# An early jump in VectorE's program and another order of GpSimd's last waits, in a layer norm that is bound by its transfers

## Chip, cores, metric

One core of one Trainium2 chip. The metric is the device time of one execution in microseconds (us), lower is better. All executions named here were fast, with a granted clock of 1.0.

## The reference

```python
def setup_inputs():
    batch, seq, dim = 32, 512, 1024
    return {"x": np.random.randn(batch, seq, dim).astype(np.float32), "eps": 1e-5}

def reference(x, eps):
    mean = np.mean(x, axis=-1, keepdims=True)
    var = np.var(x, axis=-1, keepdims=True)
    return ((x - mean) / np.sqrt(var + eps)).astype(np.float32)
```

16,384 rows of 1,024 floats: 67 MB are read and 67 MB are written.

## The kernel before

The rows go through a ring of 48 row slots in each partition, in 17 tiles (15 of 8 rows, then 6 and 2). SyncE issues the loads (ScalarE that of half the first tile), VectorE takes each row's statistics, GpSimd combines them, ScalarE takes the root, normalizes in place and issues the store. A load into a ring place waits for the store of the tile that was there. VectorE's program is three tiles, a loop of six tiles that runs twice, and the rest:

```python
    nc.vector.memset(eps_t[:], eps_val)
    nc.vector.memset(power[:], -1.0)
    for t in range(FIRST):                      # FIRST = 3
        vector(t, 16, 1)                        # 16 bn_stats and a reciprocal
    turn = nc.vector.alloc_register("turn")
    nc.vector.reg_mov(turn, 1)
    nc.vector.addr_align(128, max_nops=0)
    with nc.vector.Fori(16, 16 * TURNS + 1, 16) as arrived:
        for t in range(FIRST, FIRST + SLOTS):   # 6 tiles, TURNS = 2
            vector(t, nc.vector.lower_val(arrived), turn)
        nc.vector.reg_add(turn, turn, 1)
    for t in range(FIRST + TURNS * SLOTS, len(plan)):
        vector(t, 16, 1)
    ...
    for t in range(len(plan)):
        if t in owner.values():
            nc.gpsimd.wait_ge(stored[t], sixteens(stored, t))
```

`addr_align(n, max_nops=0)` asks that the next instruction be loaded at a multiple of n instruction slots. The gap is not filled with no-ops; a branch leads over it (in the trace of before, one COMPARE_BRANCH of VectorE's sequencer at 52.46 us, 41 ns long). The last lines are the end of the kernel: GpSimd waits for the stores that nobody else has waited for.

## Time and profile before

| | before |
|---|---|
| time, median of the first 3 runs | 318.04 us (317.63 to 318.19) |
| span of the profiled run | 316.04 us |
| time less span | 1.84 us |
| moved by DMA | 134.2 MB, 425 GB/s |
| 8 KB instruction packets in the span | 3 |
| last store: first and last of its 16 parts land | 313.67, 314.96 us |

The page counts 16 DMA engines, and the trace has 16 landing records for each transfer; I read them as one part on each engine. A wait is over with the last of the 16: of the load that the first statistics wait for, the first part landed at 12.85 us, the fifteenth at 13.36 and the last at 13.72, and the statistics start at 13.75. So one late part is enough to delay a tile.

### The profile page before, as it was taken

Reading aid. Unit: us, or ns where it says so; the run is one execution under the profiler, and the core shown is the slowest. Engines: PE = TensorE matmul, PEld = TensorE weight load, DVE = VectorE, ACT = ScalarE, POOL = GpSimd, SP = SyncE. Lnnn points to the kernel's source line nnn. Section 1 sums busy time; section 2 is a strip of 40 time slices with the busy share of each in tenths; the row PEclk is TensorE's granted clock in tenths of the full one; section 3 lists DMA queues with packets and bytes.
Section 4 is the critical chain, followed back from the end, with each engine's and each line's share of the span. In section 5 each row is a group of like instructions: output and inputs, shape, how many; then the busy total and the mean of one; then the engine's idle time right before and its main releaser. Section 6 shows DMA issues by size and latency. Waiting matters only on the chain.

```text
span 316.0 us, 713 instructions
## 1 busy us (share of the span) xinstructions
DVE 156.4 (49%) x273; ACT 153.0 (48%) x146; POOL 41.7 (13%) x176
## 2 busy tenths in 40 slices
DVE  0296595956191651907529084380934709283000
ACT  1006695865834709256091651907429083383800
POOL 0002202022002020020200202011020110204300
DMA  7999999999999999999999999999999999999996
GB/s 294 435 460 402 452 406 402 461 398 465 399 466 402 460 415 448 431 431 452 411 456 406 456 406 456 406 460 402 464 402 460 406 441 452 429 434 425 448 399 285
DMA packets 5043, 134.24 MB, mean 425 GB/s; under 512 B 560, under 2 KB 560, under 8 KB 560
## 3 DMA queue, kind: packets, MB, share of 16 engines
q10 hardware_dynamic: 2592, 69.21, 50.9%
q1 hardware_dynamic: 2448, 65.01, 47.9%
q14 instruction: 3, 0.02, 0.0%
HBM read 67.11 MB, written 67.11 MB: 425 GB/s over the span
## 4 chain that ended last, share of the span: by engine, by line
DMA 61%; DVE 18%; ACT 9%; POOL 5%; issue 2%; ACTq 0%; DVEq 0%; POOLq 0%; SPq 0%
DMA ring<-in_x_dram 32%; DMA out_dram<-ring 29%; DVE stats L119 17%; ACT ring L215 9%; POOL rstd L187 1%; POOL dev L177 1%; POOL dev L181 1%; ACT std L205 0%; POOL dev L173 0%; POOL nmean L170 0%; POOL dev L174 0%; POOL half L166 0%; POOL half L182 0%; POOL nmean L167 0%; POOL ss L183 0%
## 5 line engine op out<-in xcount | busy, mean ns | idle before, releaser
L119 DVE BATCH_NORM_STATS2 stats<-ring 128x6 f32<-128x512 f32 x256 | 153.5, 677 | 86.1 <-DMA ring<-in_x_dram 85.5
L215 ACT ACTIVATE ring<-ring,nmr,rstd 128x1024 f32<-128x1024 f32 x128 | 146.6, 1226 | 11.2 <-POOL nmr L190 11.2
L205 ACT ACTIVATE std<-ss,eps_t 128x8 f32<-128x8 f32 (+2 forms) x17 | 5.1, 300 | 135.1 <-POOL ss L183 134.7
L166 POOL TENSOR_TENSOR half<-stats 128x16 f32<-128x16 f32 (+2 forms) x17 | 4.0, 233 | 232.3 <-DVE stats L119 232.3
L130 DVE RECIPROCAL rstd<-std 128x8 f32<-128x8 f32 x15 | 3.0, 203 | 48.5 <-ACT std L205 48.5
L177 POOL TENSOR_SCALAR dev<-dev 128x32 f32<-128x32 f32 (+2 forms) x17 | 5.0, 295 | 1.5
L190 POOL TENSOR_TENSOR nmr<-nmean,rstd 128x8 f32<-128x8 f32 (+2 forms) x17 | 3.5, 205 | 9.9 <-DVE rstd L130 9.7
L181 POOL TENSOR_TENSOR dev<-dev,stats 128x32 f32<-128x32 f32 (+2 forms) x17 | 4.3, 255 | 1.4
L173 POOL TENSOR_TENSOR dev<-stats,nmean 128x32 f32<-128x32 f32 (+2 forms) x17 | 4.1, 241 | 1.4
L174 POOL TENSOR_TENSOR dev<-dev 128x32 f32<-128x32 f32 (+2 forms) x17 | 4.0, 237 | 1.3
L170 POOL TENSOR_SCALAR nmean<-nmean 128x8 f32<-128x8 f32 (+2 forms) x17 | 4.0, 235 | 1.5
L182 POOL TENSOR_TENSOR half<-dev 128x16 f32<-128x16 f32 (+2 forms) x17 | 3.7, 215 | 1.3
L167 POOL TENSOR_TENSOR nmean<-half 128x8 f32<-128x8 f32 (+2 forms) x17 | 3.4, 202 | 1.3
L183 POOL TENSOR_TENSOR ss<-half 128x8 f32<-128x8 f32 (+2 forms) x17 | 3.4, 202 | 1.3
L187 POOL TENSOR_TENSOR rstd<-std,power 128x6 f32<-128x6 f32 (+1 forms) x2 | 2.1, 1042 | 3.0 <-ACT std L205 3.0
L205 ACT ACT_TABLE_LOAD x1 | 1.3, 1283 | 1.3 <-SPq L55 1.3
L134 DVE MEMSET eps_t<- 128x1 f32 x1 | 0.1, 59 | 1.0 <-SPq L55 1.0
L251 POOL MEMSET const-float32-0.0<- 128x1 f32 x1 | 0.1, 99 | 0.2 <-issue 0.2
L251 POOL MEMSET const-bfloat16-1.0<- 128x1 bf16 x1 | 0.1, 102 | 0.0
L251 POOL MEMSET const-uint8-127<- 128x1 uint8 x1 | 0.1, 102 | 0.0
L251 POOL MEMSET const-float32-1.0<- 128x1 f32 x1 | 0.1, 99 | 0.0
L135 DVE MEMSET power<- 128x8 f32 x1 | 0.1, 65 | 0.0
## 6 DMA issues: line engine op xcount, KB each, us to landing
out_dram<-ring ACTq DMA_DIRECT2D x15, 4096.0 KB, 46.4
ring<-in_x_dram SPq DMA_DIRECT2D x14, 4096.0 KB, 45.5
ring<-in_x_dram SPq DMA_DIRECT2D x1, 3072.0 KB, 43.1
out_dram<-ring ACTq DMA_DIRECT2D x1, 3072.0 KB, 16.0
ring<-in_x_dram ACTq DMA_DIRECT2D x1, 2048.0 KB, 12.6
ring<-in_x_dram SPq DMA_DIRECT2D x1, 2048.0 KB, 12.8
ring<-in_x_dram SPq DMA_DIRECT2D x1, 1024.0 KB, 54.8
out_dram<-ring ACTq DMA_DIRECT2D x1, 1024.0 KB, 14.3
```

The costliest lines, as they stand in the source:

```text
L119: i = nc.vector.bn_stats(out=stats[:, at + k, s, :], in_=ring[:, at + k, s * BN_MAX : (s + 1) * BN_MAX],)
L166: then(0, g.tensor_tensor(out=h, in0=mean4[:, :, 0:2], in1=mean4[:, :, 2:4], op=ALU.add))
L170: g.tensor_scalar(out=nm, in0=nm, scalar1=-1.0 / H, scalar2=None, op0=ALU.mult),
L173: then(3, g.tensor_tensor(out=d, in0=mean4, in1=spread, op=ALU.add))
L174: then(4, g.tensor_mul(out=d, in0=d, in1=d))
L177: g.tensor_scalar(out=d, in0=d, scalar1=float(D // H), scalar2=None, op0=ALU.mult),
L181: then(6, g.tensor_tensor(out=d, in0=d, in1=m2, op=ALU.add))
L182: then(7, g.tensor_tensor(out=h, in0=d[:, :, 0:2], in1=d[:, :, 2:4], op=ALU.add))
L187: i = g.tensor_tensor(out=r, in0=std_t, in1=power[:, :K], op=ALU.pow)
L190: then(10, g.tensor_mul(out=nmr[:, at : at + K], in0=nm, in1=r), own)
L205: nc.scalar.activation(out=std[:, at : at + K], in_=ss[:, at : at + K], func=AF.Sqrt, bias=eps_t[:], scale=1.0 / D,)._wait_ge(*summed[t]). ...
L215: i = nc.scalar.activation(out=ring[:, k, :], in_=ring[:, k, :], func=AF.Identity, bias=nmr[:, k : k + 1], scale=rstd[:, k : k + 1],).then ...
```

## The change

The intent: VectorE's code is moved to a multiple of 64 slots at the very start, while VectorE has no data (in before it is idle there for 12.64 us). And the wait for the last store is put on GpSimd's last branch, so that no further instruction follows that landing.

```diff
     nc.vector.memset(eps_t[:], eps_val)
     nc.vector.memset(power[:], -1.0)
+
+
+    nc.vector.addr_align(64, max_nops=0)
     for t in range(FIRST):
         vector(t, 16, 1)
...
-    for t in range(len(plan)):
+    for t in reversed(range(len(plan))):
         if t in owner.values():
             nc.gpsimd.wait_ge(stored[t], sixteens(stored, t))
```

## The prediction

> **What bounds the kernel now.** I read the profile's page first, to see which resource is full. Its busy shares, its DMA row, its queues and its groups of instructions give this:
>
> ```profile
> DVE 156.4 (49%) x273; ACT 153.0 (48%) x146; POOL 41.7 (13%) x176
> ...
> DMA  7999999999999999999999999999999999999996
> ...
> q14 instruction: 3, 0.02, 0.0%
> HBM read 67.11 MB, written 67.11 MB: 425 GB/s over the span
> ...
> L119 DVE BATCH_NORM_STATS2 stats<-ring 128x6 f32<-128x512 f32 x256 | 153.5, 677 | 86.1 <-DMA ring<-in_x_dram 85.5
> ```
>
> No engine is busy for half of the span. The 16 DMA engines are at nine tenths or more in 38 of 40 slices, and 134.2 MB at 425 GB/s are 315.8 us, the whole span of 316.0. VectorE's statistics wait 85.5 us for loads. So the transfers bound the kernel. A change of the program text that moves no byte can gain only before the queues are full, after the last byte, or where it lets the queues run dry. The diff touches VectorE's code position and GpSimd's last waits, so I looked at three places: VectorE's start, its way into its loop, and the end.
>
> The timeline of the first 16 us:
>
> ```profile
> 0.93 0.37 SPq L96 DMA_DIRECT2D ring<-in_x_dram  x1
> 1.01 0.06 DVE L134 MEMSET eps_t<- 128x1 f32 x1 [1.01 <-SPq L55]
> 1.04 0.07 DVE L135 MEMSET power<- 128x8 f32 x1
> ...
> 13.75 2.47 DVE L119 BATCH_NORM_STATS2 stats<-ring 128x6 f32<-128x512 f32 x4 [12.64 <-DMA ring<-in_x_dram]
> ```
>
> The new jump will stand between the second and third of these VectorE rows: 12.64 us of idle time that a load ends.
>
> The chain of waits around the way into the loop, from the third reciprocal to the statistics of tile 3 (L140 is the alignment that the kernel already has, seen as a branch of the sequencer DVEq):
>
> ```profile
> 52.36 0.06 DVE rstd L130
> 52.42 0.03 issue
> 52.46 0.04 DVEq L140
> 52.50 0.49 issue
> 52.99 0.04 DVEq L141
> ...
> 53.15 9.60 DVE stats L119 x16
> ```
>
> The branch is recorded for 0.04 us, and nothing follows it for another 0.49. That is the one visible cost of code position. What it costs the kernel is told by the timeline after it, at the next tile:
>
> ```profile
> 65.98 0.20 DVE L130 RECIPROCAL rstd<-std 128x8 f32<-128x8 f32 x1 [3.24 <-ACT std L205]
> ...
> 66.95 1.29 DVE L119 BATCH_NORM_STATS2 stats<-ring 128x6 f32<-128x512 f32 x2 [0.76 <-DMA ring<-in_x_dram]
> ```
>
> VectorE waits again, 0.76 us, for the load of tile 4, whose last part landed at 66.92.
>
> The end, from the queries by source line (columns: shortest/median/longest ns, first and last start). L234 holds GpSimd's waits for the stores, L55 the branch out of the kernel's block and the signal after it:
>
> ```profile
> L234 POOLq EVENT_SEMAPHORE  x3: 42/43/43, 305.3 to 315.0; - x3
> ...
> L55 POOLq COMPARE_BRANCH  x1: 38/38/38, 315.1 to 315.1; - x1
> L55 POOLq NOP  x1: 17/17/17, 315.2 to 315.2; - x1
> ```
>
> In the records with three decimals: the last store's last part lands at 314.957, the third wait is recorded at 314.980, the branch at 315.067, the signal at 315.238, and the closing barriers end at 316.04.
>
> [...]ScalarE's stores land in the order of issue, each about 19.3 us after the one before in the steady part (98.89, 118.23, 137.57 us). [...] The trace shows three instruction packets inside the span, of 8,192 bytes each in the packet records, at 57.1, 84.5 and 94.3 us. It shows none at the branch of 52.46, so it does not show that this branch waited for such a fetch. [...]from a branch's start to the next recorded instruction it is 206 ns at VectorE's back edge (157.285 to 157.491) and 536 ns at L140 (52.456 to 52.992). The measured ones are used. [...]
>
> **The change part by part.** The built programs differ in just two places, line numbers aside.
>
> *VectorE.* One alignment to 64 slots is added after the two memsets; by the title it becomes one taken branch. No work moves between engines. Added cost: one branch, 0.2 to 0.54 us by the two measured ones, say 0.54, at about 1.1 us. It ends near 1.7 us, and the data comes at 13.72. Even if the target must be fetched, and if that took 5 us on full queues (a guess well beyond the 0.3 us that a packet takes), 7 us would remain. On the path: 0. Possible gain: code ahead of the loop now begins on a multiple of 64, and it is 51 instructions of tiles 0 to 2 and one register move. It ends about 12 slots short of the next multiple of 64, so the second branch skips a dozen slots[...]. If it falls from 536 ns to the back edge's 206, tile 3 starts 0.33 us earlier; if nothing changes, 0. Where does 0.33 us go? Tile 3's reciprocal moves from 65.98 to 65.65, then tile 4 still waits for its load until 66.92: VectorE's own gain ends there, and 0.76 us idle become 1.09. ScalarE's tile 3 ends 0.33 us earlier, so its store is issued at 75.36 and not 75.69. But the store of tile 2 was issued at 62.07 and lands at 98.89[...]: 23 us of slack against 0.33. The store's landing (118.23), which releases the load of tile 9, does not move. On the path: 0.
>
> *GpSimd.* The same seven waits, in the other order. They are packed two to a semaphore instruction, the seventh on the branch. Before, in pairs: tiles 14 and 13; 15 and 12; 16 and 11; on the branch tile 10. After: 12 and 13; 11 and 14; 10 and 15; on the branch tile 16. Before, the last landing releases the third semaphore instruction at 314.980 and the branch starts 87 ns later. After, the three semaphore instructions are through once tile 15's store has landed (312.53), 2.4 us ahead of the end, and the landing releases the branch itself. Removed from the path: 315.067 - 314.980 = 0.087 us, with nothing beside it, for all engines wait there. Nothing is added unless a waiting branch leaves later than one that finds its semaphore set. GpSimd's first branch, which waited too, took 153 ns to the next record (0.744 to 0.897); the last one, which did not, 171. So no penalty shows.
>
> Sum: 0 - 0.087 = -0.09 us. From 318.04 that is 317.95 us, 0.03% less.
>
> **The rivals.** (a) *The branch's stall does reach the end.* Then up to 0.33 us come on top, or 0.67 if tile 3 followed as closely as tile 1 did (119 ns from its reciprocal's start to its first statistics, against 789 at tile 3): 317.3 to 317.6. For it: the chain of waits runs through these rows. Against it: the chain follows releasers backwards and does not show slack, and the two slacks above (0.76 us on VectorE, 23 us in the store queue) are both larger than the gain. (b) *The new position costs something.* A fetch might now fall where VectorE is needed, for instance at the second branch or at the loop's exit. If it added one more 0.54 us at 52 us, the 0.76 us before tile 4 would still swallow it. At the loop's exit the wait for the next load is 3.94 us. Time unchanged, 317.95; only several us at once could show, up to 319. (c) *Code position outside the span.* The time is 317.88 where the span is 316.04; 1.8 us are not seen, and code at the end of VectorE's program lies elsewhere after the change. A few tenths either way: 317.6 to 318.4. (d) *Transfers fall differently.* [...] That would be a few tenths, of either sign.
>
> **Range and chances.** The three runs before lie between 317.63 and 318.19, a spread of 0.56 us that is six times my effect. The median of the runs after may be off by 0.3 us from this alone[...]; rival (a) widens the low side and (b), (c) the high side. I take 317.4 to 318.5. Two per cent are 6.4 us, more than all the terms together, so faster or slower by that much is 1% each.
>
> **What would show it.** Right: an early branch of VectorE near 1.1 us with the first statistics still at 13.7 and released by the load; tile 4's statistics still started by its load near 66.9 whatever the way into the loop costs; the store of tile 3 landing near 118.2; the last wait record some 2.4 us before the last landing and the branch within 30 ns after it; from landing to span's end 1.00 us in place of 1.09. Wrong: tile 9's load landing earlier by as much as the branch got shorter (then rival a); the first statistics later than 13.8 (then the fetch did not hide); a DMA row with slices below nine in the middle; or a time below 317.4 in repeated pairs of runs.

## The result, and the profile after

| | before | after |
|---|---|---|
| time, median of 6 runs | 317.78 us | 318.48 us |
| range | 317.63 to 318.19 | 317.94 to 319.39 |
| ratio of the fast runs | | 1.0021, 95% interval 1.0004 to 1.0039 |
| span of the profiled run (its time) | 316.04 (317.88) | 317.57 (319.39) |
| 8 KB instruction packets in the span | 3 | 4 |
| last store: first and last part land | 313.67, 314.96 | 313.65, 316.56 |

A ratio is the mean time of one kernel's fast runs over that of the other's in the same rounds, so it is not quite the ratio of the medians. The change is slower by 0.2%, and its runs spread 1.45 us where those of before spread 0.56. The profiled execution of after is its slowest, so the 1.5 us between the two spans is the largest case and not the mean; the mean is 0.0021 x 317.8 = 0.7 us.

The page of after, the rows of the DMA engines, of the instruction queue and of the statistics:

```profile
DMA  7999999999999999999999999999999999999995
...
q14 instruction: 4, 0.03, 0.0%
HBM read 67.11 MB, written 67.11 MB: 423 GB/s over the span
...
L119 DVE BATCH_NORM_STATS2 stats<-ring 128x6 f32<-128x512 f32 x256 | 153.5, 677 | 87.6 <-DMA ring<-in_x_dram 87.1
```

No work on an engine grew. VectorE waits 87.1 us for loads where it waited 85.5. There is one more instruction packet. Where it is, the DMA view of after, restricted to the first 14 us, says (the same view of before has no q14 row):

```profile
## 3 DMA queue, kind: packets, MB, share of 16 engines
q1 hardware_dynamic: 175, 3.11, 52.3%
q10 hardware_dynamic: 144, 2.10, 39.9%
q14 instruction: 1, 0.01, 0.1%
```

The timeline of after at the start, then the query of L138, the new alignment (shortest/median/longest ns, first and last start):

```profile
1.04 0.07 DVE L135 MEMSET power<- 128x8 f32 x1
...
14.30 1.88 DVE L119 BATCH_NORM_STATS2 stats<-ring 128x6 f32<-128x512 f32 x3 [13.19 <-DMA ring<-in_x_dram]
```

```profile
L138 DVEq COMPARE_BRANCH  x1: 47/47/47, 1.0 to 1.0; - x1
```

The jump is at 1.03 us as intended, and the first statistics are still started by the load. But that load is late: its last part lands at 14.28 us where it landed at 13.72, while the first part lands at 12.95 against 12.85. One part of the 16 is late: behind the first there are 0.36 us to the fifteenth and 1.32 to the sixteenth (before: 0.51 and 0.88).

The way into the loop, in the chain of after, and tile 4's start in its timeline:

```profile
52.92 0.06 DVE rstd L130
52.98 0.04 issue
53.01 0.04 DVEq L143
53.05 0.46 issue
53.52 0.04 DVEq L144
...
53.68 9.60 DVE stats L119 x16
```

```profile
67.73 1.88 DVE L119 BATCH_NORM_STATS2 stats<-ring 128x6 f32<-128x512 f32 x3 [1.02 <-DMA ring<-in_x_dram]
```

The second branch costs what it cost (0.50 us from its start to the next record, 0.54 before), and tile 4 is still started by its load.

The last 18 us in the DMA view, before and then after (40 slices of 0.45 us from 300 us on; the second row is GB/s):

```profile
DMA  9599195193939393939393926999962000000000
GB/s 874 218 510 583 73 874 218 73 728 164 710 164 710 164 710 164 710 164 710 164 710 164 710 109 291 455 401 401 473 291 91 36 0 0 0 0 0 0 18 0
```

```profile
DMA  9899899779969595959595959699973200000000
GB/s 437 364 510 510 364 510 437 328 328 401 492 291 601 218 655 218 655 218 655 218 655 218 655 218 401 273 473 382 492 310 146 91 18 18 36 18 0 0 0 0
```

The full rates end near the same place. After the change four slices follow with 18, 18, 36 and 18 GB/s: single packets of 8 KB, one after the other. I read this as one DMA engine that still has its part of the last store to write while fifteen are done: 15 of the 16 parts have landed by 314.85 us (before 314.66), the last lands at 316.56. (The lone 18 near the end of the row of before is an instruction packet at 317.2 us, after the span.)

GpSimd's end, from the queries by line:

```profile
L237 POOLq EVENT_SEMAPHORE  x3: 43/7212/7218, 299.6 to 306.9; - x3
...
L55 POOLq COMPARE_BRANCH  x1: 38/38/38, 316.6 to 316.6; - x1
```

Each of these instructions waits for two stores (two semaphores in its record). The last of the three now starts at 306.9 and ends with its second store's landing at 314.11, and the last landing at 316.564 releases the branch itself at 316.588. From landing to the span's end it takes 1.001 us, before 1.087. This part works, and is worth 0.086 us.

**Following one DMA engine.** The records give each packet's start, duration, size and queue, but not its DMA engine. I sorted the packets into 16 sequences, with two demands: the next packet of a sequence starts about 3 ns before the end of the last (in the records of before and after nearly every packet has an end 3 to 4 ns behind its start), and every sequence carries the same bytes. This assignment is mine; where packets end within a few ns of each other it can swap two sequences, which shows as a wrong count between two completions. The after trace has one such swap that matters, at 32 us, which I undid by these counts. All 13 traces were sorted again, with one more demand: every sequence ends its part of each transfer with one of the 4-byte packets in the records (560 in before, 16 for each of the 35 transfers). It gave the same bytes on all 16 sequences of a trace (but for one packet in threejumps_tt), both of after's fetches below on one sequence, and in every run that has more than one fetch of VectorE's, all of them on one. Around the new packet (4.829 us) and around the one at 57.9, on what comes out as the same sequence:

```
start us   took ns   bytes   what
 4.829      309       8192   instruction fetch
 5.135     1142      16384   load packet behind it (611 ns is the median of this size)
57.914      309       8192   instruction fetch
58.220     1747      32768   packet behind it (1213 ns is the median of this size)
```

By these rows a fetch of VectorE's code costs the engine that carries it about 306 + 531 = 837 ns, and 306 + 534 = 840 ns: its own packet, and a packet behind it that takes longer. In the trace of before one fetch, at 57.132, has the same cost (1751 ns behind it), and its sequence is the last to end. In after there are two on one sequence. It ends at 316.24 us; the middle sequence ends at 313.78.

### The profile page after: what moved, and what is told of

Same layout as the page of the kernel before. It is cut to its first block, busy times and chain, and to the rows that moved or that the text cites. A ratio compares the mean times of both kernels' runs of the same rounds, so it can differ in the third digit from the quotient of the medians.

```text
span 317.6 us, 714 instructions
## 1 busy us (share of the span) xinstructions
DVE 156.4 (49%) x273; ACT 153.0 (48%) x146; POOL 41.7 (13%) x176
## 4 chain that ended last, share of the span: by engine, by line
DMA 61%; DVE 17%; ACT 9%; POOL 5%; issue 2%; ACTq 0%; DVEq 0%; POOLq 0%; SPq 0%
DMA ring<-in_x_dram 32%; DMA out_dram<-ring 29%; DVE stats L119 17%; ACT ring L218 9%; POOL rstd L190 1%; POOL dev L180 1%; POOL dev L184 1%; ACT std L208 0%; POOL dev L176 0%; POOL nmean L173 0%; POOL dev L177 0%; POOL half L169 0%; POOL half L185 0%; POOL nmean L170 0%; POOL ss L186 0%
## 5 line engine op out<-in xcount | busy, mean ns | idle before, releaser
L119 DVE BATCH_NORM_STATS2 stats<-ring 128x6 f32<-128x512 f32 x256 | 153.5, 677 | 87.6 <-DMA ring<-in_x_dram 87.1
```

Source lines behind the costliest of these rows:

```text
L119: i = nc.vector.bn_stats(out=stats[:, at + k, s, :], in_=ring[:, at + k, s * BN_MAX : (s + 1) * BN_MAX],)
```

## The experiments

**Theory A**, a supposition that the runs are to test. Each further stretch of 128 instruction slots that an engine's program enters (a line, in the expectations) draws one fetch of 8,192 bytes. All fetches of one compute engine's code go by the same DMA engine, 0.84 us each, as read from after above. As every transfer waits for the last of its 16 parts and the DMA engines are at nine tenths or more in 38 of 40 slices, this delay is kept to the end. **Rivals:** B, the reversed waits are what costs; C, the spread of runs; D, VectorE's own stall or its code position; E, only a fetch among the first loads costs; F, the taken branch itself; G, the number of fetches in all, wherever they go.

All experiments are edits of a stand-in that uses a constant tile. Diffs below are against the stand-in. The runs are in three groups, each on one chip with the kernel before run beside it (medians 317.83, 317.75 and 317.80 us). The stand-in ran in the first group alone; in the others a kernel is compared by its ratio to the kernel before, which the stand-in equals.

### base_tt, the stand-in

```diff
-            g.tensor_scalar(out=nm, in0=nm, scalar1=-1.0 / H, scalar2=None, op0=ALU.mult),
+            g.tensor_mul(out=nm, in0=nm, in1=by_h[:, :K]),
...
-            g.tensor_scalar(out=d, in0=d, scalar1=float(D // H), scalar2=None, op0=ALU.mult),
+            g.tensor_mul(out=d, in0=d, in1=by_n[:, :K]),
...
+    g.memset(by_h[:], -1.0 / H).then_inc(filled, 1)
+    g.memset(by_n[:], float(D // H)).then_inc(filled, 1)
+    g.wait_ge(filled, 2)
```

> The stand-in for the kernel before: its two GpSimd multiplications by a constant are made with a constant tile instead of a scalar operand, since that form alone may be run again; nothing else moves. All theories: same time as the kernel before within 0.15%, instruction packets in the span 3, one of them within 6 us after VectorE's branch at 52.5 us.

Measured: 317.82 us (317.49 to 318.35), ratio 1.0000 (0.9986 to 1.0014), 3 packets, the first at 56.9 us. It may stand for the kernel before.

### both_tt, jump_tt, waits_tt: the two parts together and alone

both_tt has the diff of the change; jump_tt has its first part alone, waits_tt its second.

> Both parts of the change on the stand-in. Theory A (one more 8 KB instruction fetch of VectorE falls on the DMA engine that already carries its other one; each costs that engine 0.31 us for its own packet and about 0.53 us in the packet behind it, and every transfer waits for the slowest engine): 4 instruction packets, the last one of the 16 parts of a store lands 2 to 3 us after the first in place of 1.3, time 0.4 to 1.2 us over the stand-in. Theory B (the reversed waits make the end slower): also 0.4 to 1.2 us over, but the time from last landing to span's end grows over 1.09 us. Theory C (the difference is the spread between runs): within 0.2 us of the stand-in.

> The early jump alone, waits in the old order. A: as slow as both parts together, within 0.1 us, 4 instruction packets. B: equal to the stand-in within 0.2 us. C: equal to the stand-in within 0.2 us.

> The reversed waits alone. A: 0.09 us under the stand-in (the span from last landing to end 1.00 us in place of 1.09), 3 instruction packets. B: 0.4 to 1.2 us over the stand-in. C: equal within 0.2 us.

| | median us | ratio to the kernel before (95%) | packets | last landing to end |
|---|---|---|---|---|
| both_tt | 318.32 | 1.0018 (1.0004 to 1.0031) | 4 | 1.00 us |
| jump_tt | 318.65 | 1.0017 (1.0003 to 1.0030) | 4 | 1.08 us |
| waits_tt | 317.69 | 0.9998 (0.9984 to 1.0012) | 3 | 1.00 us |

The slowdown comes back on another chip and is wholly that of the jump: 0.0017 x 317.8 = 0.54 us. B falls. C falls by the intervals, which leave 1 out with both kernels that have the jump and hold it with both that don't. (The page of jump_tt counts 5 instruction packets; one of them has 24 bytes, at 0.09 us.) The gain of the waits is seen in the trace and is too small for the runs to show.

### threejumps_tt: a larger dose

```diff
     nc.vector.memset(power[:], -1.0)
+    nc.vector.addr_align(64, max_nops=0)
+    nc.vector.memset(z1[:], 0.0)
+    nc.vector.addr_align(128, max_nops=0)
+    nc.vector.memset(z2[:], 0.0)
+    nc.vector.addr_align(128, max_nops=0)
```

> Three early jumps in a row instead of one (to multiples of 64, 128 and 128 slots, a small memset between them), all done by some 10 us while VectorE has no data. Theory A (each new stretch of 128 slots that VectorE enters draws an 8 KB fetch, always on the same DMA engine, 0.85 us of delay for it each): 5 or 6 instruction packets in the span, of them 3 or 4 VectorE's on one engine, 1.3 to 2.6 us over the stand-in. Rival D (the early jump costs by a VectorE effect, such as a stall at its first statistics or a later loop entry): first statistics move from 13.7 us, no growth beyond the one jump's 0.5 to 0.8. Rival E (only the first fetch matters, since it falls in the first loads): 0.5 to 0.8 us over the stand-in, whatever the number of packets.

Measured: 320.77 us (four runs, 320.45 to 321.13), ratio 1.0094 (1.0079 to 1.0109), that is +3.0 us, more than I had put for A at most. The page's instruction row, and VectorE's timeline of the first 20 us:

```profile
q14 instruction: 6, 0.05, 0.0%
```

```profile
1.61 0.06 DVE L139 MEMSET z<- 128x1 f32 x1 [0.49 <-issue]
5.80 0.06 DVE L141 MEMSET z<- 128x1 f32 x1 [4.13 <-issue]
14.85 5.44 DVE L121 BATCH_NORM_STATS2 stats<-ring 128x6 f32<-128x512 f32 x9 [8.98 <-DMA ring<-in_x_dram]
```

VectorE waits here, for its code as I read it: 4.13 us between the second jump and what follows it. Yet from 5.86 us on it has nothing to do until the load lands at 14.82, so this stall is hidden, and D does not explain the time. The load is late by about 1 us. In the reconstruction the four packets of VectorE (3.98, 9.71, 15.57, 58.91 us) are on one sequence, which ends 3.8 us behind the middle one. Read as above, they cost it 0.84, 0.98, 0.98 and 0.84 us, 3.6 in all. The landing records say the same without any sorting: 15 parts of the last store have landed by 315.05 us, the 16th lands at 317.95.

One more thing is in these lines. The memset behind the first jump ran at 1.61 us, before the first fetch began at 3.98: it did not wait for that fetch. The fetch, then, seems to be for the code after it.

### hop8_tt: a taken branch of at most 7 slots

```diff
     nc.vector.memset(power[:], -1.0)
+    nc.vector.addr_align(8, max_nops=0)
```

> A taken branch of at most 7 slots at the same place as the early jump. A: the time follows the packets and not the branch. If the shift leaves tiles 0 to 2 in the first 128 slots, 3 packets and the stand-in's time within 0.2 us; if it pushes their end over a 128 line, 4 packets, VectorE's two within some us of each other near 50 to 57 us, and 0.4 to 0.9 us over. Rival F (a taken branch at the start costs by itself): 0.4 to 0.9 us over with 3 packets.

Measured: 317.98 us, ratio 1.0008 (0.9995 to 1.0022), 3 packets. The branch is in the trace at 1.05 us, as in the change. No slowdown clear of noise; but the interval reaches 0.7 us and so doesn't exclude F's 0.4. The traces speak against F: without a further fetch 15 parts of the last store land by 314.71 us and the 16th at 315.00 (before 314.66 and 314.96), while in the runs with further fetches of VectorE the 16th alone is late. So it is where the code lands that costs, as far as this shows, not the jump.

### noalign_tt: no alignment at all

```diff
-    nc.vector.addr_align(128, max_nops=0)
```

> No alignment at all, not even the one ahead of the loop. A: VectorE passes a 128 line in sequence once, so 3 packets and the stand-in's time within 0.3 us, unless the line falls inside the loop and is entered again at each turn: then one more packet for each entry and 0.5 us or more over. Under rival D the missing 0.5 us stall before tile 3 makes it faster by 0.3 us.

Measured: 318.28 us, ratio 1.0018 (1.0005 to 1.0032), 3 packets. I had expected the stand-in's time. The cores' spans agree with that (316.0 to 316.4 us in its five runs, 315.7 to 316.5 for the stand-in). What grew is outside the span: time less span is 2.15 to 2.20 us here and 1.75 to 1.88 in all runs of the others, the change included. Only VectorE's code position differs, so this is a second effect of position, 0.36 us after the last recorded instruction; what happens there the trace doesn't show. (The records of the stand-in have one more 8 KB instruction packet 1.2 us after the span; here it is missing, but in jumpfree_tt too, which has no such cost.) So the alignment ahead of the loop, with its 0.5 us stall at 52.5 us, is worth keeping in the kernel before, for the position that it gives; jumpfree_tt lacks it without this loss. The stall's absence did not shorten the span, against D.

### jumpfree_tt: the early jump, no alignment ahead of the loop

```diff
     nc.vector.memset(power[:], -1.0)
+    nc.vector.addr_align(64, max_nops=0)
...
-    nc.vector.addr_align(128, max_nops=0)
```

> The early jump, but the loop follows without the second alignment. A: the early fetch is the same; the loop is 104 slots long and starts 52 slots behind a multiple of 64, so it lies across a 128 line and enters it in each turn: 4 to 6 packets in the span, 0.5 to 2 us over the stand-in. If the early fetch was the only further one that is needed and code that was fetched stays, 3 packets and the time of the stand-in. Rival E: 0.5 to 0.8 us over in each case.

Measured: 318.19 us, ratio 1.0013 (1.0000 to 1.0027), 4 packets: VectorE's are at 5.4 and 110.9 us, on one sequence, which ends 1.6 us behind the middle. The second one came inside the loop, in the fourth of its six tiles (begun at 105.2 us). With the stretches of theory A, which the trace doesn't show, I estimate: had the early jump gone to slot 64, the loop would begin near slot 116 and meet the multiple of 128 in its first tile, near 57 us. Gone to 128, it begins near 180, and the next multiple is some 76 slots into it, in the fifth tile (tile 7, begun at 125.5 us), and the packet came one tile ahead of that. The second estimate is the nearer one. The second pass drew no further packet. The interval touches 1, so the time alone would not decide.

### late_tt: the further jump late

```diff
     for t in range(FIRST):
+        if t == 2:
+            nc.vector.addr_align(128, max_nops=0)
         vector(t, 16, 1)
```

> The further 128-slot line is entered late: the added alignment (to 128) stands ahead of tile 2, at about 39.5 us, not at the start, and the loop then lies in the next line. A: the moment doesn't matter, 4 instruction packets, VectorE's two (near 44 and 57 us) on one DMA engine that ends about 1.7 us behind the middle one, 0.4 to 0.9 us over the stand-in (317.8). Rival E (only a fetch among the first loads costs): within 0.2 us of the stand-in.

Measured: 318.61 us, ratio 1.0029 (1.0015 to 1.0043), 4 packets, VectorE's at 44.8 and 56.4 us on one sequence, which ends 1.5 us behind the middle. E falls: two fetches well after the first loads cost as well. If anything the late one costs more than the early one of jump_tt (1.0029 against 1.0017, with intervals that overlap), and the sequences suggest why: an early delay is partly made up. VectorE's sequence was 1.00 us behind the middle at 15 us and 0.69 at 41 us in jump_tt, 0.74 and 0.40 in both_tt; in between, around 40 us, all sequences have packets that take longer (of 32 KB in after, up to 2.25 us, where the median is 1.21), and VectorE's loses least there (0.31 us in jump_tt, the others 0.45 to 0.74). After that the delay was kept (in before 1.16 us at 79 us, 1.07 at the end). Theory A's "kept to the end" is too strong for a fetch among the first loads.

### sp1_tt, sp3_tt: the same fetches on another compute engine

```diff
             dma._wait_ge(stored[gone[-1]], sixteens(stored, gone[-1]))
+        if t == 5:              # sp3_tt: if 5 <= t <= 7
+            nc.sync.addr_align(128, max_nops=0)
```

> One further fetch on an engine that has none: SyncE jumps to the next multiple of 128 slots after it has issued tile 5's load; VectorE is as before. A (what counts is the sum on the worst DMA engine, and each engine's code comes by its own DMA engine): 4 instruction packets, but on four DMA engines, so within 0.2 us of the stand-in. Rival G (what counts is the number of fetches in all): 0.4 to 0.9 us over, as with the early jump of VectorE.

> SyncE jumps three times, after the loads of tiles 5, 6 and 7. A: 6 instruction packets, three of them on one DMA engine that VectorE's isn't, this engine ends 1.6 to 2.5 us behind the middle one, time 0.7 to 1.6 us over the stand-in. Rival D (the cost comes from VectorE's own stall or from code position): within 0.2 us. Rival G: 1.5 to 2.5 us over.

| | median us | ratio to the kernel before (95%) | packets | last sequence ends behind the middle one |
|---|---|---|---|---|
| sp1_tt | 317.96 | 1.0006 (0.9992 to 1.0020) | 4 | 0.9 us |
| sp3_tt | 319.27 | 1.0044 (1.0030 to 1.0058) | 6 | 2.4 us |

sp1_tt has as many packets as the change, and no slowdown clear of noise: by the sorting, its fourth is on a DMA engine that had none. Its interval alone, up to 0.64 us, doesn't exclude G's 0.4. But sp3_tt and threejumps_tt have 6 packets each, and their intervals, 1.0030 to 1.0058 and 1.0079 to 1.0109, lie apart: G falls by them. sp3_tt puts three on that engine and is slower by 0.0044 x 317.8 = 1.4 us, with VectorE's program as it was. So D falls as the cause of the change's slowdown: the same loss is had without touching VectorE, by loading one DMA engine. Nor are SyncE's loads late as a whole: 15 parts of the last store land by 314.69 us (before 314.66), the 16th at 316.53.

The size is not that of theory A. SyncE's three fetches cost their sequence 0.60, 0.58 and 0.58 us, not 0.84. Two of them more should add 1.16 us, and from sp1_tt to sp3_tt it is 0.0038 x 317.8 = 1.2 us. The rest of the 2.4 us is not fetches: in both runs this sequence falls back by about 0.8 us more after 100 us, in packets that take some ns longer; the cause stays open.

## Why the prediction was right or wrong

- **The bound** was read rightly: the transfers, on all 16 DMA engines, at nine tenths or more in 38 of 40 slices. The time, 318.48 us, lies 0.02 us inside the upper end of the range, by luck: that side was kept wide for rivals (b), (c) and the spread, and neither rival is what happened. The sign of the change was wrong.
- **The early jump, "On the path: 0"**: this is the step that failed. As a stall of VectorE it was right: the jump stands where I put it and the first statistics are still released by the load. Nor was my 5 us for a fetch too short: in after its packet begins 3.8 us after the jump (1.03 to 4.83) and takes 0.31. But I treated the fetch only as something VectorE may have to wait for. It is also a DMA packet, and so adds work to the resource that I had just named as the bound. In place of 0 the term is +0.54 us by jump_tt's ratio, from 0.84 us on one DMA engine. It is less than 0.84 because an early delay is partly made up (late_tt) and because VectorE's sequence is not the last one in every run without the jump (in base_tt another ended 0.03 us later, in hop8_tt 0.44). The first statistics came at 14.30 and not 13.7, which I had listed as a sign of failure, though for another reason: not VectorE's code was late, its data was.
- **What misled me**: I had the three packets before my eyes and set them against 134 MB. As a share of 16 engines they are nothing. They should be read per engine: 0.84 us out of one engine's 312 busy us (98.8% of 316.04, the shares of the two queues) is 0.27%, and the last part sets the time: in after 15 parts of the last store have landed by 314.85 us, the 16th at 316.56.
- **The second branch**: 0.50 us and not the 0.21 that I allowed for; no gain, and none was on the path. The slack worked as argued: tile 4 still waits 1.02 us for its load.
- **The store of tile 3, "The store's landing (118.23) ... does not move"**: its first part doesn't (117.48, before 117.53), its last does (119.76; nine of the 16 land after 118.3), and that is the part that the next load waits for: it is issued at 119.78 us, in before at 118.24.
- **The waits, -0.087 us**: right, 1.087 to 1.001 us in the trace; waits_tt shows it again without the jump. But the prediction took a wait's record to start with the landing that releases it. That fits the third wait of before (314.980 us, landing at 314.957) and not after: two of the three records there last 7.2 us and end, not start, at a landing (the last at 314.14, landing at 314.11). So the last wait's record ends 2.4 us before the last landing, as forecast of its start.
- **Rival (c), position outside the span**, is real in noalign_tt (0.36 us) but not in the change, where 1.8 us remain. Rival (b), "a fetch might now fall where VectorE is needed", named the fetch but looked for it on the wrong engine. Rival (a) is refuted by the same slack.
- **The spread.** I said that the runs' spread was six times my effect, and the change itself widened it. The traces suggest why: the DMA engine that carries VectorE's code starts ahead of or behind the others by some tenths of a us. In the profiled run of after it was 0.17 us behind at 4 us and in that of both_tt 0.13 ahead, and it ended 2.5 and 1.1 us behind the middle. A further 0.6 us near 79 us, largest in after, is a slow packet on the same sequence (at 79.34 us in after, 1.92 us, where the median of its size is 1.21); its cause stays open.

Of the versions run none beats the kernel before clear of noise. The one that the experiments point to is the reversed waits without the jump (waits_tt): 0.09 us in the trace, a ratio of 0.9998 in the runs.

## What to carry to other kernels

In this kernel, with its DMA engines at nine tenths or more in 38 of 40 slices, the last of the 16 parts set when a tile was there, so one fetch of 8 KB, of 134 MB in all, cost 0.54 us (jump_tt), and three more of SyncE's code on one sequence 1.4 us (sp3_tt). Where a trace shows the same bound, read anything that adds a transfer on the DMA engine that takes it, however small its share of all bytes. Code was such a transfer here; a jump that was hidden for VectorE was not hidden for the DMA engine that fetched the code. If a program has to be moved about in memory, count the further instruction packets that each engine's jumps draw: each added jump to a multiple of 64 or 128 slots drew one here (one in jump_tt and late_tt, three in threejumps_tt and sp3_tt), the one of at most 7 slots none (hop8_tt). Two or more of one engine's on one sequence cost time (late_tt 1.0029, sp3_tt 1.0044, threejumps_tt 1.0094; in jumpfree_tt, 1.0013, the interval touches 1); one on a sequence that had none did not clear the noise (sp1_tt 1.0006).
